# A decoder block's first MLP projection with stacked operands, its opening in smaller steps, and one merge step placed two background steps later

## The chip, the cores and the metric

The kernel runs on one core of a Trainium2 chip. The metric is the device time of one execution in microseconds (us), the median of several runs. TensorE appears in the profile as PE (matmuls) and PEld (loads of the stationary operand), VectorE as DVE, ScalarE as ACT, GpSimd as POOL; SP issues most transfers.

## The reference

One layer of a hybrid decoder trunk on 256 tokens of width 2048, with a memory of 256 tokens, all in float32:

```
proj = rmsnorm(x) @ w_in            # q,k,v,gates of three branches, 3 x 2048 merge gates
oa, ob = gated_deltanet(...), hgrn2(...)
oc = memory_attention(cq, rmsnorm(mem), w_kv)
merged = ga*(oa @ w_br_a) + gb*(ob @ w_br_b) + gc*(oc @ w_br_c)
x = x + rmsnorm(merged @ w_out)
h2 = rmsnorm(x)
m = square(relu(h2 @ w_mlp_in)) @ w_mlp_out     # 2048 -> 8192 -> 2048
x = x + rmsnorm(m)
```

## The kernel before

**Precision by splitting.** Every float32 operand of a large product is split into a rounded part and a remainder (hi and lo, both float32r), and a product is the sum of three matmuls: hi·hi, hi·lo and lo·hi. Weights arrive by `load_w` (L137): one DMA of two k-tiles by 512 columns (512 KB) on SP's queue, a cast on ACT to `wh` (L144), and a subtraction on DVE to `wl` (L146). The pools `w`, `wh` and `wl` have four buffers each, so a load, a cast or a subtraction waits for the one four groups earlier to be done with.

**Units.** `unit` (L154) computes 512 output columns for all 256 tokens. It goes over the k-tiles in groups of two. In kind "x" the activations are stationary and the weights move: per k-tile and block of 128 tokens three matmuls that each move 512 columns (L180, L181, L182). In kind "w" the weights are stationary and the activations move: per k-tile and block of 128 output columns three matmuls that each move 256 tokens (L187, L188, L189), so the output comes transposed, as the next product needs it. An x unit over 16 k-tiles has 96 matmuls, a w unit 192. Both accumulate in one PSUM tile of two banks from a pool of two (`pmm`), or, with `split`, in two tiles of one bank each from the pool `pbp` of four banks that the transposes also use.

**Order of the work.** The program is written as units in sequence, with generators (`bg`) as background work: after each group `tick` runs as many background steps as a rate says, one step lasting to the next `yield`. Within that, a scheduler sets the order of each engine's instructions; PE, ACT and DVE each work through theirs in order.

**The opening** (L223 to L409): four units compute the memory's values (two x units) and keys (two w units). During the first of them `load_mem` (L241) brings `mem` in four chunks of 512 columns and `transpose_chunk` (L208) transposes each into `memh` and `meml` (L216, L200, L201). Then `gen_start` (L316) forms the norm of `mem`, loads `x` in four chunks and some small parameters, forms the sum of squares of `x` (L311), scales `x` by its norm (L373) and transposes it (L216) into `hh` and `hl`; `gen_masks` (L260) builds masks. All later projections need `hh` and `hl`.

**Merge.** In `branch` (L780), when a merged chunk `mg` is complete (L792), `gen_merge` (L767) transposes it (L774) in two background steps. The product with `w_out` needs all four chunks.

**MLP.** `mlp_in` (L1002) makes 1024 hidden columns in two units, `mlp_out` (L1047) multiplies them back in four x units over 8 k-tiles and adds into `yacc`. This is done eight times, `mlp_in(e)` ahead of `mlp_out(e-1)`. Of the 16 units of `mlp_in` the first is an x unit, the other 15 are w units: L187 to L189 with the operands `h2h` and `h2l`. Each ends with relu on ACT (L1008), a squaring on DVE (L1010), a cast on ACT (L205) and a subtraction on DVE (L206).

Of the kernel before, what the change touches and what calls it, by code (L numbers as in the profile page):

```python
# [41 lines left out]
def tile_trunk(ctx: ExitStack, tc, a):  # L42
# [4 lines left out]
    wp = ctx.enter_context(tc.tile_pool(name="wp", bufs=4))  # L47
    hp = ctx.enter_context(tc.tile_pool(name="hp", bufs=8))
    gp = ctx.enter_context(tc.tile_pool(name="gp", bufs=25))
# [9 lines left out]
    def nm(s):  # L59
        cnt[0] += 1  # L60
        return f"{s}_{cnt[0]}"
# [3 lines left out]

    def h4(name):
        return hp.tile([P, 4, S], F32R, tag="h", name=nm(name))

# [12 lines left out]

    warm = const("warm", [P, 16])
    V.memset(warm, 0.0)
    A.copy(warm, warm)
    ident = const("ident", [P, P])
# [24 lines left out]

    load_gcol(["g_mem"], 0, nc.sync.dma_start)

# [41 lines left out]
    def unit(kind, act, nk, src, c0, r0=0, pre=None, order=None, split=False, post=None):  # L154
# [52 lines left out]

    def transpose_chunk(src, tiles, c, col0):  # L208

        hi, lo = tiles  # L210
        for half in range(2):
            pt = bank("tr")
            for q in range(2):
                for t in range(NT):
                    kk = half * 2 + q
                    T.transpose(pt[:, q * S + t * P:q * S + (t + 1) * P],  # L216
                                src[:, t, kk * P:(kk + 1) * P], ident)
# [23 lines left out]
    def load_mem(k0):  # L241
        if k0 % 4:
            return
        c = k0 // 4
        t = g4("mem", (P, NT, 512))
        nc.sync.dma_start(t, mem_r[:, :, c * 512:(c + 1) * 512])
        hi, lo = g4("memh", (P, 4, S), F32R), g4("meml", (P, 4, S), F32R)
        transpose_chunk(t, (hi, lo), c, 0)
        mem_s.append(t)
        memT.append((hi, lo))  # L250

# [53 lines left out]

    def sumsq(chunks, name):
        st = small(name, 8)
        for c, t in enumerate(chunks):
            for k in range(NT):
                j = g4("junk")  # L310
                A.activation(j[:, 0:512], t[:, k, :], AF.Square, accum_out=st[:, k * 4 + c:k * 4 + c + 1])  # L311
        ss = small(name + "s", NT)
        V.tensor_reduce(out=ss, in_=st.rearrange("p (k c) -> p k c", k=NT), axis=AX.X, op=ALU.add)
        return ss

    def gen_start():  # L316
        ss = sumsq(mem_s, "ssm")
        yield
        r = rstd_of(ss, NT, D)
        V.tensor_copy(rsm, r)  # L320
# [7 lines left out]
        xs = []  # L328
        for c in range(4):
            t = g4("x", (P, NT, 512))  # L330
            nc.sync.dma_start(t, x_r[:, :, c * 512:(c + 1) * 512])
            xs.append(t)
        yield
        load_gcol(["g_pre_mix", "g_pre_mlp"], 16, adma)
        crow = const("crow", [96, P])
# [3 lines left out]
        V.tensor_copy(ccol, pc[:, 0:96])  # L339
        yield  # L340
        lrow = const("lrow", [8, P])
        adma(lrow, a["lb_raw"][0].rearrange("(c p) -> c p", p=P))
        pl = bank("pl")
        T.transpose(pl[:, 0:8], lrow, ident[0:8, 0:8])
# [18 lines left out]
        adma(alog, a["a_log"][0:1, :].to_broadcast([P, 8]))  # L363
        adma(dtb, a["dt_bias"][0:1, :].to_broadcast([P, 8]))
        A.activation(alog, alog, AF.Exp)
        yield
        ssx = sumsq(xs, "ssx")
        yield
        rx = rstd_of(ssx, NT, D)
        for c in range(4):  # L370
            hT[c] = (h4("hh"), h4("hl"))
            for t in range(NT):
                V.tensor_scalar(out=xs[c][:, t, :], in0=xs[c][:, t, :], scalar1=rx[:, t:t + 1],  # L373
                                scalar2=None, op0=ALU.mult)
            transpose_chunk(xs[c], hT[c], c, 16)
            yield

    ccol = const("ccol", [P, 96])
# [8 lines left out]
    for u in range(2):  # L387
        ps = unit("x", act_of(memT), KT, w_kv, 1024 + 512 * u, pre=load_mem if u == 0 else None)
        if u == 0:
            bg.append(gen_start())  # L390
            bg.append(gen_masks())
# [374 lines left out]

    def gen_merge(j):  # L767
        hi, lo = g4("mgh", (P, 4, S), F32R), g4("mgl", (P, 4, S), F32R)
        for hh in range(2):
# [166 lines left out]
    last = [(g, None) for g in range(4)] + [(g, t) for t in range(NT) for g in range(4, 8)]  # L936
    h2T = []

# [23 lines left out]
    for c in range(4):  # L962
        y = g4("y1", (P, NT, 512))
        ys.append(y)
        if c < 3:
            ps = unit("x", mact, KT, a["w_out"][0], 512 * c)
            for t in range(NT):
                mix_evac(y, c, t, ps[:, t * 512:(t + 1) * 512])
        else:
            h2T.extend((h4("h2h"), h4("h2l")) for _ in range(4))  # L970
# [31 lines left out]
    def mlp_in(e):  # L1002
        mt = []
        for u in range(2):
            kind = "x" if e == 0 and u == 0 else "w"
            ps = unit(kind, h2act, KT, a["w_mlp_in"][0], e * 1024 + u * 512, order=first if kind == "x" else None)
            r = g4("relu")
            A.activation(r, ps, AF.Relu)  # L1008
            hi, lo = g4("mh", (P, 4, S), F32R), g4("ml", (P, 4, S), F32R)
            V.scalar_tensor_tensor(out=r, in0=ps, scalar=0.0, in1=r, op0=ALU.max, op1=ALU.mult)  # L1010
            if kind == "x":
                for hh in range(2):
# [34 lines left out]
    def mlp_out(e, mt):  # L1047
        for c in range(4):
            args = ("x", act_of(mt), 8, a["w_mlp_out"][0], c * 512, e * 8)
            if e == NE - 1 and c == 3:  # L1050
# [5 lines left out]
                continue  # L1056
            ps = unit(*args)
            if e == 0:
                yacc[c] = g4("yacc", (P, NT, 512))
                A.copy(yacc[c], ps.rearrange("p (t n) -> p t n", t=NT))  # L1060
            elif e < NE - 1:
                V.tensor_tensor(out=yacc[c], in0=ps.rearrange("p (t n) -> p t n", t=NT), in1=yacc[c], op=ALU.add)
            else:
                for t in range(NT):
                    mlp_evac(c, t, ps[:, t * 512:(t + 1) * 512])

# [22 lines left out]
```

## Time and profile before

| what | value |
|---|---|
| runs | 1867.44, 1868.84, 1868.90 us; median 1868.84 |
| the profiled execution | 1866.51 us; span 1864.8 us from first to last instruction |
| mean granted TensorE clock | 0.996 of full |
| PE busy | 1831.4 us (98%), 11174 matmuls |
| PEld busy | 1641.5 us (88%) |
| DVE busy | 1088.3 us (58%) |
| ACT busy | 895.2 us (48%) |
| POOL busy | 45.5 us (2%) |
| moved by DMA | 333.63 MB, mean 179 GB/s |

The times in the rows of a profile are from the start of the span. Matmuls overlap, so the duration of one (0.28 us, say) is longer than the distance to the next; what a matmul costs in a stream is read from the distance of two starts. The page's line PEclk gives the clock that TensorE was granted, in tenths of full speed.

### The profile page before, as it was taken

The page shows a single profiled execution, that of the slowest core. Times are in us where ns is not written, and L with a number is a line of the kernel's source. Part 1 is how long each engine was busy: PE and PEld are TensorE (multiplying, and loading weights), DVE is VectorE, ACT ScalarE, POOL GpSimd, SP SyncE. Part 2 cuts the span into 40 slices and gives each one's busy share as a digit, 9 for nine tenths or more (in the row PEclk, how much of TensorE's full clock was granted, in tenths as well). Part 3 has the DMA queues.
Part 4 walks back from the last instruction along what each step waited for, and adds up shares of the span by engine and source line. Part 5 has one row for each costly group of instructions (what it writes and reads, how often), then busy time and mean ns, then how long its engine had stood idle before and what let it go on. Part 6 is the DMA issues. An engine that isn't in the chain of part 4 may idle for free.

```text
span 1864.8 us, 27445 instructions
## 1 busy us (share of the span) xinstructions
PE 1831.4 (98%) x11174; PEld 1641.5 (88%) x11174; DVE 1088.3 (58%) x1328; ACT 895.2 (48%) x1079; POOL 45.5 (2%) x70
## 2 busy tenths in 40 slices
PE   7899999999999999999999999999999999999997
PEld 6799999988899898888888787989898989898986
DVE  4655577764863685875455557554555554545556
ACT  5544555444545565654444445544444444444433
POOL 1100000200110000000000000000000000000000
PEclk9899999999999999999999999999999999999999
DMA  6566656664584555555665765656566655666653
GB/s 206 183 192 172 169 148 171 181 183 124 169 210 132 157 169 148 161 155 179 187 196 183 247 193 178 184 186 189 191 187 190 189 189 184 192 183 193 185 194 127
DMA packets 174383, 333.63 MB, mean 179 GB/s; under 512 B 13080, under 2 KB 13744, under 8 KB 174000
## 3 DMA queue, kind: packets, MB, share of 16 engines
q1 hardware_dynamic: 168736, 325.11, 57.7%
q10 hardware_dynamic: 4496, 4.54, 0.8%
q0 software_dynamic: 1024, 2.23, 0.6%
q8 instruction: 87, 1.43, 0.3%
q14 instruction: 40, 0.33, 0.1%
HBM read 329.60 MB, written 2.23 MB: 178 GB/s over the span
## 4 chain that ended last, share of the span: by engine, by line
PE 58%; issue 39%; DVE 2%; DMA 0%; ACT 0%; POOL 0%; SPq 0%; DVEq 0%; POOLq 0%; ACTq 0%
PE mm L180 12%; PE mm L182 12%; PE mm L181 12%; PE mm L187 6%; PE mm L189 6%; PE mm L188 5%; PE pa L865 1%; PE pw L696 1%; PE pzt L701 1%; DMA mem<-in_mem 0%; DVE wl L146 0%; PE tr L216 0%; DVE x L1044 0%; PE ab L483 0%; PE mgT L774 0%
## 5 line engine op out<-in xcount | busy, mean ns | idle before, releaser
L146 DVE TENSOR_TENSOR wl<-w,wh 128x1024 fp32r<-128x1024 f32 x608 | 741.5, 1223 | 620.7 <-ACT wh L144 619.8
L144 ACT CAST wh<-w 128x1024 fp32r<-128x1024 f32 x608 | 636.9, 1050 | 838.7 <-PE mm L182 447.6
L187 PE MATMUL mm<-h2h,wh 128*128 128x256 f32 x960 | 271.7, 283 | 0.0
L188 PE MATMUL mm<-h2l,wh 128*128 128x256 f32 x960 | 271.7, 283 | 0.0
L189 PE MATMUL mm<-h2h,wl 128*128 128x256 f32 x960 | 271.7, 283 | 0.0
L180 PE MATMUL mm<-wh,hh 128*128 128x512 f32 x576 | 228.5, 397 | 0.0
L182 PE MATMUL mm<-wh,hl 128*128 128x512 f32 x576 | 224.9, 390 | 0.0
L181 PE MATMUL mm<-wl,hh 128*128 128x512 f32 x576 | 224.5, 390 | 0.0
L187 PE MATMUL mm<-hh,wh 128*128 128x256 f32 x768 | 218.8, 285 | 0.0
L189 PE MATMUL mm<-hh,wl 128*128 128x256 f32 x768 | 217.4, 283 | 0.1
L188 PE MATMUL mm<-hl,wh 128*128 128x256 f32 x768 | 217.3, 283 | 0.0
L180 PE MATMUL mm<-wh,mh 128*128 128x512 f32 x512 | 199.3, 389 | 0.0
L181 PE MATMUL mm<-wl,mh 128*128 128x512 f32 x512 | 199.3, 389 | 0.0
L182 PE MATMUL mm<-wh,ml 128*128 128x512 f32 x512 | 199.2, 389 | 0.0
L188 PEld LDWEIGHTS mm<-h2l,wh 128*128 128x128 f32 x960 | 184.3, 192 | 0.3
L187 PEld LDWEIGHTS mm<-h2h,wh 128*128 128x128 f32 x960 | 184.3, 192 | 0.3
L189 PEld LDWEIGHTS mm<-h2h,wl 128*128 128x128 f32 x960 | 184.3, 192 | 0.0
L187 PEld LDWEIGHTS mm<-hh,wh 128*128 128x128 f32 x768 | 147.3, 192 | 0.2
L188 PEld LDWEIGHTS mm<-hl,wh 128*128 128x128 f32 x768 | 147.3, 192 | 0.2
L189 PEld LDWEIGHTS mm<-hh,wl 128*128 128x128 f32 x768 | 147.2, 192 | 0.3 <-DVE wl L146 0.3
L182 PEld LDWEIGHTS mm<-wh,hl 128*128 128x128 f32 x576 | 108.1, 188 | 23.1
L181 PEld LDWEIGHTS mm<-wl,hh 128*128 128x128 f32 x576 | 108.4, 188 | 20.9
(360 smaller groups left out, 2359.6 us busy)
## 6 DMA issues: line engine op xcount, KB each, us to landing
w<-in_w_in SPq DMA_DIRECT2D x240, 512.0 KB, 3.7
w<-in_w_mlp_in SPq DMA_DIRECT2D x128, 512.0 KB, 3.7
w<-in_w_mlp_out SPq DMA_DIRECT2D x128, 512.0 KB, 3.6
w<-in_w_kv_mem SPq DMA_DIRECT2D x32, 512.0 KB, 5.6
w<-in_w_out SPq DMA_DIRECT2D x32, 512.0 KB, 3.7
w<-in_w_br_c SPq DMA_DIRECT2D x16, 512.0 KB, 4.4
w<-in_w_br_a SPq DMA_DIRECT2D x16, 512.0 KB, 3.7
w<-in_w_br_b SPq DMA_DIRECT2D x16, 512.0 KB, 3.6
```

Of the source, the lines that this page charges most:

```text
L144: i_hi = A.copy(wh[:, 0:n, 0:width], w[:, 0:n, 0:width])
L146: i_lo = V.tensor_tensor(out=wl[:, 0:n, 0:width], in0=w[:, 0:n, 0:width], in1=wh.bitcast(F32)[:, 0:n, 0:width], op=ALU.subtract)
L180: T.matmul(o, st, wh[:, j, :], start=kt == 0, stop=False)
L181: T.matmul(o, st, wl[:, j, :], start=False, stop=False)
L182: T.matmul(o, sl, wh[:, j, :], start=False, stop=kt == nk - 1)
L187: T.matmul(o, sh, ah, start=kt == 0 and c % 2 == 0, stop=False)
L188: T.matmul(o, sh, al, start=False, stop=False)
L189: T.matmul(o, sl, ah, start=False, stop=kt == nk - 1 and c % 2 == 1)
L696: T.matmul(pw[:, b * 64:(b + 1) * 64], U[:, b, :], half_view(X, s, False)[:, b], start=True, stop=True)
L701: T.matmul(pzt[:, b * 64:(b + 1) * 64], W[:, b, :], half_view(XT, s, True)[:, b], start=True, stop=True)
L865: T.matmul(pa[:, b * 64:(b + 1) * 64], kp[:, h, t * P:(t + 1) * P], qp[:, b * 64:(b + 1) * 64], start=True, stop=True)
```

## The change

Three things change. **First**, the 15 w units of `mlp_in` become `unit_stacked`. The hi and lo parts of an activation chunk now lie in one tile (`h8`, shape 128 x 2 x 4 x 256; half as many buffers of twice the size), so that one matmul with `wh` stationary moves both, 512 columns, into a whole bank: hi·hi in its first half, hi·lo in its second. A second matmul with `wl` moves the 256 columns of the hi part into the first half. The four blocks of output columns take a bank each, alternately the four of `pbp` and the two double ones of `pmm`. The two halves are added at the end by ACT and DVE, in place of relu on ACT. The first two of the four units of each `mlp_out` now take their banks from `pbp`, and their results are evacuated by blocks of 128 tokens.

```
+    def unit_stacked(pairs, nk, src, c0, ps):
+        for g in range(nk // KG):
+            k0 = g * KG
+            wh, wl = load_w(src, k0, KG, c0)
+            for j in range(KG):
+                kt = k0 + j
+                both = pairs[kt // 4][:, :, kt % 4, :]
+                for c in range(4):
+                    T.matmul(ps[c], wh[:, j, c * P:(c + 1) * P], both, start=kt == 0, stop=False)
+                    T.matmul(ps[c][:, 0:S], wl[:, j, c * P:(c + 1) * P], both[:, 0, :], start=False, stop=kt == nk - 1)
+            tick()
...
-                split_psum(r.rearrange("p (c s) -> p c s", c=4), hi, lo)
+                if u == 0:
+                    ps = [bank("mm") for _ in range(4)]
+                else:
+                    ps = []
+                    for _ in range(2):
+                        both = pmm.tile([P, 1024], F32, tag="mm", name=nm("mm"))
+                        ps.extend((both[:, 0:512], both[:, 512:1024]))
+                unit_stacked(h2B, KT, a["w_mlp_in"][0], c0, ps)
+                r4 = r.rearrange("p (c s) -> p c s", c=4)
+                for c in range(4):
+                    A.copy(r4[:, c, :], ps[c][:, S:2 * S])
+                    V.tensor_tensor(out=r4[:, c, :], in0=ps[c][:, 0:S], in1=r4[:, c, :], op=ALU.add)
+                V.scalar_tensor_tensor(out=r, in0=r, scalar=0.0, in1=r, op0=ALU.max, op1=ALU.mult)
+                split_psum(r4, hi, lo)
...
-            ps = unit(*args)
+            ps = unit(*args, split=c < 2)
```

**Second**, the opening. The first chunk of `mem` comes in two halves by two DMAs, and every chunk is transposed in two calls, one per half. The load of `g_mem` goes from SP's queue to ACT's, ahead of ACT's table load. The sums of squares of `x` are formed chunk by chunk in steps of their own, the chunks of `x` are loaded one per step, the mask steps alternate with them, and each chunk is scaled one step ahead of its transposes.

```
-        ssx = sumsq(xs, "ssx")
-        yield
-        rx = rstd_of(ssx, NT, D)
+        load_x()
+        sumsq_chunk(xs[0], st, 0)
+        yield
...
+        next(masks)
+        yield
...
+        sumsq_chunk(xs[3], st, 3)
+        yield
+        next(masks)
+        yield
+        rx = rstd_of(sumsq_of(st, "ssx"), NT, D)
...
+        scale(0)
+        yield
         for c in range(4):
-            hT[c] = (h4("hh"), h4("hl"))
+            if c < 3:
+                scale(c + 1)
+            hc = h8("hh")
+            hT[c] = (hc[:, 0], hc[:, 1])
             transpose_chunk(xs[c], hT[c], c, 16)
             yield
+        yield from masks
```

ACT, second chunk of `mem` (tile `mem_185` before, `mem_186` now; `tr` are its transposes in PSUM, `memh` the hi part). Before:

```order
8 L144 CAST wh_169<-w_167 128x1024
9 L144 CAST wh_209<-w_207 128x1024
10 L200 ACTIVATE memh_187<-tr_189,gcol 128x256
11 L144 CAST wh_227<-w_225 128x1024
12 L200 ACTIVATE memh_187<-tr_189,gcol 128x256
13 L144 CAST wh_267<-w_265 128x1024
14 L200 ACTIVATE memh_187<-tr_198,gcol 128x256 x2
```

The same place of ACT's program now:

```order
9 L145 CAST wh_170<-w_168 128x1024
10 L145 CAST wh_201<-w_199 128x1024
11 L145 CAST wh_228<-w_226 128x1024
12 L145 CAST wh_259<-w_257 128x1024
13 L145 CAST wh_286<-w_284 128x1024
14 L215 ACTIVATE memh_187<-tr_190,gcol 128x256
15 L215 ACTIVATE memh_187<-tr_217,gcol 128x256
```

The four activations that make `memh` of the second chunk stood among the casts, and now stand behind the casts of the fifth and sixth weight group. On PE, seven of the chunk's eight transposes stood ahead of the first chunk's matmuls, and two do now.

PE, the transposes of `x` (L216, chunks `x_416` and `x_418`), inside the second values unit (`mm_397`, last two weight groups). Before:

```order
193 L180 MATMUL mm_397<-wh_599,memh_303 128x512
194 L216 MATMUL tr_579<-ident,x_416 128x128
195 L216 MATMUL tr_588<-ident,x_416 128x128
196 L181 MATMUL mm_397<-wl_601,memh_303 128x512
197 L216 MATMUL tr_579<-ident,x_416 128x128 x3
198 L216 MATMUL tr_588<-ident,x_416 128x128 x3
199 L182 MATMUL mm_397<-wh_599,meml_304 128x512
200 L216 MATMUL tr_619<-ident,x_418 128x128 x4
201 L216 MATMUL tr_628<-ident,x_418 128x128 x4
202 L180 MATMUL mm_397<-wh_639,memh_303 128x512
```

PE now, the first chunk of `x` (`x_417`), inside the first keys unit (`mm_617`, last two weight groups):

```order
350 L189 MATMUL mm_617<-meml_246,wh_798 128x256
351 L190 MATMUL mm_617<-memh_245,wl_800 128x256
352 L231 MATMUL tr_829<-ident,x_417 128x128 x4
353 L231 MATMUL tr_838<-ident,x_417 128x128 x4
354 L188 MATMUL mm_617<-memh_303,wh_849 128x256
355 L189 MATMUL mm_617<-meml_304,wh_849 128x256
```

The transposes of `x` have moved out of the second values unit into the two keys units, eight at a time with 24 matmuls of a weight group between two batches.

**Third**, the generator for the last merged chunk begins with two empty steps.

```
     def gen_merge(j):
+        if j == 3:
+            yield
+            yield
```

PE, the end of the last branch unit (`mm_9332`, later `mm_9329`) and the start of the first `w_out` unit (`mm_9421`, later `mm_9418`). Before:

```order
5521 L182 MATMUL mm_9332<-wh_9389,ol_8196 128x512
5522 L180 MATMUL mm_9421<-wh_9424,mgh_8712 128x512
5523 L774 MATMUL mgT_9460<-ident,mg_5375 128x128 x4
5524 L774 MATMUL mgT_9485<-ident,mg_5375 128x128 x4
5525 L181 MATMUL mm_9421<-wl_9426,mgh_8712 128x512
```

The same place now:

```order
5489 L183 MATMUL mm_9329<-wh_9386,ol_8193 128x512
5490 L181 MATMUL mm_9418<-wh_9421,mgh_8709 128x512
5491 L825 MATMUL mgT_9493<-ident,mg_5372 128x128 x4
5492 L825 MATMUL mgT_9518<-ident,mg_5372 128x128 x4
5493 L182 MATMUL mm_9418<-wl_9423,mgh_8709 128x512
```

On PE nothing has moved here: the eight transposes still stand behind the first matmul of the `w_out` unit. On ACT the two casts that follow them stand behind one weight cast more, and on DVE the first of the two subtractions does.

More of the change, by code (lines that the diff above doesn't have):

```diff
@@ L64, in g4, with h8 @@
         return gp.tile(list(shape), dt, tag="g", name=nm(name))
-    def h4(name):
-        return hp.tile([P, 4, S], F32R, tag="h", name=nm(name))
+    def h8(name):
+        return hp.tile([P, 2, 4, S], F32R, tag="h", name=nm(name))
     def small(name, n=16):
@@ L109, in load_gcol @@
         V.tensor_copy(gcol[:, c0:c0 + n], pg[:, 0:n])
-    load_gcol(["g_mem"], 0, nc.sync.dma_start)
+    load_gcol(["g_mem"], 0, adma)
+    warm = const("warm", [P, 16])
+    V.memset(warm, 0.0)
+    A.copy(warm, warm)
     bg = []
@@ L206, in split_psum, with transpose_chunk @@
         V.tensor_tensor(out=lo, in0=ps, in1=hi.bitcast(F32), op=ALU.subtract)
-    def transpose_chunk(src, tiles, c, col0):
+    def transpose_chunk(src, tiles, c, col0, halves=(0, 1)):
         hi, lo = tiles
-        for half in range(2):
+        for half in halves:
             pt = bank("tr")
@@ L241, in load_mem @@
     def load_mem(k0):
[L242 to L250, printed above, removed]
+        c, half = k0 // 4, k0 % 4 // 2
+        if half == 0:
+            mem_s.append(g4("mem", (P, NT, 512)))
+            memT.append((g4("memh", (P, 4, S), F32R), g4("meml", (P, 4, S), F32R)))
+        t = mem_s[c]
+        cols = [slice(half * 256, half * 256 + 256)] if c == 0 else [slice(0, 512)] * (1 - half)
+        for sl in cols:
+            nc.sync.dma_start(t[:, :, sl], mem_r[:, :, c * 512 + sl.start:c * 512 + sl.stop])
+        transpose_chunk(t, memT[c], c, 0, (half,))
     mgt, mlt, caus = const("mgt", [P, P]), const("mlt", [P, P]), const("caus", [P, P])
@@ L304, in tile_trunk, with sumsq_chunk, sumsq_of @@
     hT = [None] * 4
[L306 to L311, printed above, removed]
+    def sumsq_chunk(t, st, c):
+        for k in range(NT):
+            j = g4("junk")
+            A.activation(j[:, 0:512], t[:, k, :], AF.Square, accum_out=st[:, k * 4 + c:k * 4 + c + 1])
+    def sumsq_of(st, name):
         ss = small(name + "s", NT)
@@ L316, in gen_start @@
     def gen_start():
-        ss = sumsq(mem_s, "ssm")
+        st = small("ssm", 8)
+        for c, t in enumerate(mem_s):
+            sumsq_chunk(t, st, c)
         yield
-        r = rstd_of(ss, NT, D)
+        r = rstd_of(sumsq_of(st, "ssm"), NT, D)
         V.tensor_copy(rsm, r)
@@ L328, in gen_start, with load_x @@
         xs = []
-        for c in range(4):
+        def load_x():
+            c = len(xs)
             t = g4("x", (P, NT, 512))
@@ L364, in gen_start, with scale @@
         adma(dtb, a["dt_bias"][0:1, :].to_broadcast([P, 8]))
+        yield
+        st = small("ssx", 8)
+        load_x()
+        sumsq_chunk(xs[0], st, 0)
+        yield
         A.activation(alog, alog, AF.Exp)
+        next(masks)
         yield
-        ssx = sumsq(xs, "ssx")
+        load_x()
+        sumsq_chunk(xs[1], st, 1)
         yield
-        rx = rstd_of(ssx, NT, D)
-        for c in range(4):
-            hT[c] = (h4("hh"), h4("hl"))
+        next(masks)
+        yield
+        sumsq_chunk(xs[2], st, 2)
+        yield
+        next(masks)
+        yield
+        sumsq_chunk(xs[3], st, 3)
+        yield
+        next(masks)
+        yield
+        rx = rstd_of(sumsq_of(st, "ssx"), NT, D)
+        def scale(c):
             for t in range(NT):
@@ L969, in tile_trunk @@
         else:
-            h2T.extend((h4("h2h"), h4("h2l")) for _ in range(4))
+            h2B.extend(h8("h2h") for _ in range(4))
+            h2T.extend((b[:, 0], b[:, 1]) for b in h2B)
             ps = unit("x", mact, KT, a["w_out"][0], 512 * c, order=last, split=True,
@@ L1004, in mlp_in @@
         for u in range(2):
-            kind = "x" if e == 0 and u == 0 else "w"
-            ps = unit(kind, h2act, KT, a["w_mlp_in"][0], e * 1024 + u * 512, order=first if kind == "x" else None)
+            c0 = e * 1024 + u * 512
+            hi, lo = g4("mh", (P, 4, S), F32R), g4("ml", (P, 4, S), F32R)
             r = g4("relu")
[L1008 to L1011, printed above, removed]
+            if e == 0 and u == 0:
+                ps = unit("x", h2act, KT, a["w_mlp_in"][0], c0, order=first)
+                A.activation(r, ps, AF.Relu)
+                V.scalar_tensor_tensor(out=r, in0=ps, scalar=0.0, in1=r, op0=ALU.max, op1=ALU.mult)
                 for hh in range(2):
```

31 lines of the change are left out of this document (18 added, 13 removed).

## The prediction

> **What bounds the kernel now.** I read the page first: busy times and the chain that ended last.
>
> ```profile
> span 1864.8 us, 27445 instructions
> PE 1831.4 (98%) x11174; PEld 1641.5 (88%) x11174; DVE 1088.3 (58%) x1328; ACT 895.2 (48%) x1079; POOL 45.5 (2%) x70
> PE 58%; issue 39%; DVE 2%; DMA 0%; ACT 0%; POOL 0%; SPq 0%; DVEq 0%; POOLq 0%; ACTq 0%
> ```
>
> PE is busy for 98% of the span, and the chain is PE and its issue for 97%. So two things count: what PE's stream costs, and where PE stands still. Next, the stream in the timeline of PE: first and last start of a run of 54 narrow matmuls (256 columns, 18 triples of an MLP w unit), then of 93 wide ones (512 columns, 31 triples of an x unit).
>
> ```profile
> 1214.64 0.28 PE L187 MATMUL mm<-h2h,wh 128*128 128x256 f32 x1
> ...
> 1221.12 0.28 PE L187 MATMUL mm<-h2h,wh 128*128 128x256 f32 x1
> ```
>
> ```profile
> 1499.97 0.39 PE L180 MATMUL mm<-wh,mh 128*128 128x512 f32 x1
> ...
> 1521.05 0.39 PE L180 MATMUL mm<-wh,mh 128*128 128x512 f32 x1
> ```
>
> Narrow: 6.48 us / 54 = 0.1200 us from start to start. Wide: 21.08 / 93 = 0.2267. Two narrow ones cost 0.2400 for the same 512 columns, so a straight line through both prices has 0.0133 us per instruction that no column pays for.
>
> Then, where PE stands still: its waits, the windows around them, and PE's timeline on both sides of the longest.
>
> ```profile
> PE tr L216 <- DMA mem<-in_mem: 5.0, 2, 2.8
> PE tr L216 <- issue: 4.9, 2, 3.9
> ...
> PE mgT L774 <- DVE mg L792: 2.4, 1, 2.4
> ...
> PE mT L1017 <- DVE relu L1010: 0.7, 1, 0.7
> ```
>
> ```profile
> 60.90:84.13 23.23, 16.98 (x92) 15.17 (x92) 17.18 (x38) 15.72 (x32) 0.71 (x1) 0.78 0.25 89
> 84.13:124.80 40.67, 40.67 (x341) 40.67 (x341) 25.07 (x33) 15.73 (x15) 4.33 (x6) 1.00 0.68 208
> ```
>
> ```profile
> 60.70 0.39 PE L180 MATMUL mm<-wh,memh 128*128 128x512 f32 x1
> 64.98 0.66 PE L216 MATMUL tr<-ident,x 128*128 128x128 f32 x2 [3.89 <-issue]
> ...
> 80.93 0.41 PE L189 MATMUL mm<-memh,wl 128*128 128x256 f32 x1
> 81.14 0.41 PE L187 MATMUL mm<-memh,wh 128*128 128x256 f32 x1
> ```
>
> All waits of note lie in the opening, but for one of 2.4 us at the last merged chunk. The stretch from 60.90 to 84.13 is the bad one: the mean granted clock is 0.78 there, and behind each standstill matmuls start at 0.21 instead of 0.12. From 84.13 on PE is full.
>
> **The stacked projection.** A w unit has 16 x 4 = 64 triples. Each becomes one wide and one narrow matmul: 0.2267 + 0.1200 = 0.3467 us for 0.3600. 15 units x 64 x 0.0133 = **12.8 us less**, all on the path, since PE is the bound here. The trace has no alternation of wide and narrow, so I bound it. Nothing gained if the wide one, whose moving operand is now two pieces 4 KB apart, is priced as two narrow ones (0.3600). At the other end the narrow one costs half a wide one (0.1133): 960 x 0.0200 = 19.2 us. I take the straight line, since an operand in two pieces already runs at its price, the Gram matmuls with a moving operand of 2 x 128 columns:
>
> ```profile
> 328.47 0.28 PE L417 MATMUL kk<-kqh 128*128 128x256 f32 x1
> 328.59 0.28 PE L418 MATMUL kk<-kql,kqh 128*128 128x256 f32 x1
> ```
>
> 0.12 us, as in one piece. [...]
>
> The end of a unit gets heavier. What it costs now, the nearest rows for 256 columns out of PSUM, and how full ACT and DVE are in such a unit (third and fourth busy time behind the length):
>
> ```profile
> L1010 DVE SCALAR_TENSOR_TENSOR relu<-mm,relu 128x1024 f32<-128x1024 f32 x16 | 19.5, 1217 | 0.0
> L206 DVE TENSOR_TENSOR ml<-relu,mh 128x1024 fp32r<-128x1024 f32 x15 | 18.3, 1218 | 0.0
> L1008 ACT ACTIVATE relu<-mm 128x1024 f32<-128x1024 f32 x16 | 16.4, 1022 | 0.0
> L205 ACT CAST mh<-relu 128x1024 fp32r<-128x1024 f32 x15 | 15.7, 1046 | 0.0
> ...
> L522 DVE SCALAR_TENSOR_TENSOR cv<-mm,ccol,cv 128x255 f32<-128x255 f32 x24 | 11.5, 478 | 3.3 <-ACT cv L519 3.2
> ...
> L519 ACT ACTIVATE cv<-mm,ccol 128x256 f32<-128x256 f32 x24 | 11.3, 472 | 5.4 <-DVE cv L522 5.4
> ```
>
> ```profile
> 1206.00:1229.00 23.00, 23.00 (x194) 23.00 (x193) 12.07 (x10) 10.26 (x10) 0.00 (x0) 1.00 0.58 186
> ```
>
> ACT goes from 1.02 + 1.05 to 4 x 0.47 + 1.05 = 2.93 us (+0.9), DVE from 2.44 to 4 x 0.48 + 2.44 = 4.35 (+1.9). Of 23 us, 13 and 11 are idle, so I cost it at nothing. Queued behind these instructions are the casts and subtractions for the next groups, but three groups (3 x 8 x 0.3467 = 8.3 us of PE) lie ready in the four buffers, and the added chain is some 5.4 us (1.88 + 1.22 + 1.05 + 1.22). The banks change hands as well: a stacked unit takes all four of `pbp` or both tiles of `pmm`, and the unit after it takes the other pool, so each has a whole unit to be emptied. One exception is the first stacked unit, which needs the tile that the x unit ahead of it just filled; there PE's order has seven pairs (2.4 us) and the transposes of `relu` first, and the wait of before (0.7 us, on `mT`) stays what it was. The evacuation of `mlp_out` in halves is the same work in more instructions under the same cover. In the stretch between `w_out` and the MLP a few rows of ACT and DVE change places; its waits were small, and I put ±1 us on it.
>
> **The opening, transposes of `x`.** At full rate the stretch from 60.90 to 84.13 holds 32 transposes, 14 wide and 46 narrow matmuls (92 in all). A batch of eight transposes takes 0.87 us:
>
> ```profile
> 406.32 0.87 PE XT L689 x8
> ```
>
> 32 x 0.109 + 14 x 0.2267 + 46 x 0.12 = 12.2 us; 11.1 of the 23.2 are lost. The cause is on ACT and DVE (timelines): ACT waits for a parameter's DMA, then forms all eight squares ahead of the next casts, and DVE can scale `x` only behind them.
>
> ```profile
> 55.45 0.21 ACT L365 ACTIVATE alog<-alog 128x8 f32<-128x8 f32 x1 [4.36 <-DMA alog<-in_a_log]
> ...
> 58.08 0.62 ACT L311 ACTIVATE junk<-x 128x512 f32<-128x512 f32 x1
> ...
> 63.08 2.92 ACT L144 CAST wh<-w 128x1024 fp32r<-128x1024 f32 x3
> ```
>
> ```profile
> 64.40 1.68 DVE L373 TENSOR_SCALAR x<-x,r 128x512 f32<-128x512 f32 x4 [0.82 <-POOL r L228]
> ```
>
> PE stood in its order before a transpose of `x` from 61 to 64.98. Now the transposes come one to two units later, when `x` has long been scaled, so that wait and those behind it go. What is late next: the ACT wait for `alog` stays, and four squares instead of eight stand ahead of the cast for the last group of the second values unit. The eight took 63.08 - 58.08 = 5.0 us, so that cast begins at about 58.08 + 2.5 = 60.6, and with 1.05 for itself and 1.23 for its subtraction all is ready at 62.9. PE wants it at 60.70 + 3 x 0.2267 = 61.4 and can do one matmul without the subtraction: 1.3 us lost. Four switches to transposes and back cost 0.1 each. Gain 11.1 - 1.3 - 0.4 = **9.4 us** (5 if the heavy DVE stretch of the keys units, with all `hl`, holds up each batch by 1 us; 11 if nothing is late).
>
> **The opening, chunks of `mem`.** PE's timeline at the second chunk:
>
> ```profile
> 13.06 1.75 PE L216 MATMUL tr<-ident,mem 128*128 128x128 f32 x7 [2.19 <-DMA mem<-in_mem]
> ...
> 20.42 0.27 PE L216 MATMUL tr<-ident,mem 128*128 128x128 f32 x1
> 20.45 0.48 PE L180 MATMUL mm<-wh,memh 128*128 128x512 f32 x1
> ```
>
> It will still land at about 13 us: the same bytes stand ahead of it on SP's queue, and the `g_mem` row that left the queue is small. At 20.4 PE lost nearly nothing, since seven transposes were done. Now six of the eight come there, and the activations behind two casts that wait for PE, as those of the third chunk did before:
>
> ```profile
> 26.00 1.04 PE L216 MATMUL tr<-ident,mem 128*128 128x128 f32 x8
> 26.25 1.05 ACT L144 CAST wh<-w 128x1024 fp32r<-128x1024 f32 x1 [1.68 <-PE mm L182]
> ...
> 29.00 0.51 PE L182 MATMUL mm<-wh,meml 128*128 128x512 f32 x1 [0.55 <-DVE meml L201]
> ```
>
> From 26.00 to 29.00 PE did eight transposes and two matmuls, 0.87 + 0.45 = 1.3 us of work: 1.7 lost. So **1.7 us more** (0 to 3). The third chunk's DMA moves on SP behind four more weight loads, the last of which waits for a buffer:
>
> ```profile
> 20.28 0.37 SPq L139 DMA_DIRECT2D w<-in_w_kv_mem  x1
> ```
>
> ```profile
> 3.83 9.18 DMA mem<-in_mem
> ```
>
> The first row is the ninth weight load; the chunk goes out right behind it, at some 20.8, and is wanted at 26.00 + 1.7 = 27.7, so 6.9 us cover it. The second row, from the chain, is the transfer of the second chunk: 9.2 us in the crowd of the start. At 20 us less is under way, so I count nothing, and put up to 2 us into the range.
>
> **The merged chunk.** The 2.4 us wait stays: on PE its transposes stand where they stood, behind the first matmul of `w_out`. 0 us; 2.4 less only if the order were another.
>
> **Sum.** -12.8 - 9.4 + 1.7 = -20.5 us. The profiled execution took 1866.51 us (span 1864.8), 2.3 below the median of the runs, 1868.84; from that median the forecast is **1848.3 us**.
>
> **Rivals.** (1) *The projection gains nothing*: the two-piece operand makes a wide matmul two narrow ones, or the fixed part is not per instruction. Against it is the Gram row; for it, no alternating stream in the trace. Then only the opening counts: 1868.8 - 7.7 = 1861.1. Chance 0.07. [...] (2) *The opening gives back what it saves*: PE still stands before a transpose of `x`, or the late third chunk takes a new wait at 26 to 30 us and the clock falls as at 61. For it: DVE is the fullest engine there. 1868.8 - 12.8 = 1856. Chance 0.12. (3) *Slower*: PE waits at the start of each of the 15 stacked units or of the unit behind for the banks, which now take eight instructions (4 copies at 0.47 and the last addition, 2.4 us) to empty. 15 x 2.4 = 36 us, 1884; it decides from 20.5 / 15 = 1.4 us per unit. Against it: the pools alternate. Chance 0.03.
>
> **How the numbers follow.** The forecast and its near variants have 0.78. Low end: projection 16 and opening 10.5, 1842; high end: opening at its small end and rival (2), and a little over, 1858; beyond lie rivals (1) and (3) and part of the unknown price. About 0.2% (3.7 us) is what a measurement of this kernel can tell from no change, so "same" is 1865.1 to 1872.6: only (1) and (2) together get there, 0.03 out of their chances. Slower is rival (3), 0.03; faster 0.94.
>
> **What would show it.** In the projection: starts of wide matmuls 0.347 apart from pair to pair, 22.2 us per unit, PE without a gap at unit ends. In the opening: no wait of 3.9 us on a transpose, clock 1.00 between 20 and 115 us, a stall of some 1.7 us at 20 us and one near 62, and the first use of `hh` at about 117 instead of 124.9:
>
> ```profile
> 124.91 0.28 PE L187 MATMUL mm<-hh,wh 128*128 128x256 f32 x1
> ```
>
> A wait of 2.4 us on `mgT` remains. Wrong would be pairs at 0.36, a clock under 1.0 between 60 and 115 us, or waits for PSUM at unit ends.

## The result, and the profile after

| | runs (us) | median | against before |
|---|---|---|---|
| before | 1867.44, 1868.39, 1868.84, 1868.90 | 1868.62 | |
| after | 1851.34, 1852.16, 1855.03, 1856.05 | 1853.6 | 0.9921 [0.9904, 0.9938] |

The change makes the kernel 15.0 us faster where 20.5 were forecast. The profiled execution of after took 1855.03 us, span 1853.3, which is 11.5 less than the span of before; it is one of the two longer runs of after, for which the record has a mean granted clock of 0.997 and 0.996, against 0.998 in the two shorter ones. First the sums: busy times of the page, then the waits of PE.

```profile
PE 1822.6 (98%) x10214; PEld 1588.2 (86%) x10214; DVE 1111.0 (60%) x1412; ACT 901.6 (49%) x1128; POOL 44.2 (2%) x70
```

```profile
PE tr L231 <- DMA mem<-in_mem: 4.3, 3, 2.3
PE gcol L106 <- DMA grow<-in_g_mem: 4.0, 1, 4.0
PE mgT L825 <- DVE mg L843: 2.4, 1, 2.4
PE mT L1069 <- DVE relu L1063: 2.1, 1, 2.1
PE mm L181 <- ACT wh L145: 1.9, 1, 1.9
PE mm L182 <- DVE wl L147: 1.8, 2, 1.6
```

PE has 960 matmuls fewer and is as full as before. The wait of 3.9 us on a transpose of `x` is gone, the 2.4 us on `mgT` are there as before, and the wait on `mT` has grown from 0.7 to 2.1 us. Of the 1.8 us on `wl`, 1.6 are one wait in the first unit of the MLP, at 1129.67 us, where before had 0.65. No wait stands at the ends of the stacked units: from 1160 us on PE never stands still for more than 0.06 us.

Next, the opening: a window of PE from 60 us to the first use of `hh` (busy times, then granted clock, DMA share and GB/s), and that first use, 124.91 in before.

```profile
60.00:117.40 57.40, 57.40 (x452) 56.02 (x451) 40.91 (x67) 33.60 (x56) 3.76 (x7) 1.00 0.65 210
```

```profile
117.47 0.28 PE L188 MATMUL mm<-hh,wh 128*128 128x256 f32 x1
```

PE is busy in all of it at full clock: 7.4 us won, 7.7 forecast.

Last, the stacked stream. PE's timeline at two places, the first and last wide matmul of 31 in the first stretch of pairs and of 30 in the second:

```profile
1189.57 0.40 PE L206 MATMUL mm<-h2h,wh 128*128 128x512 f32 x1
...
1199.97 0.40 PE L206 MATMUL mm<-h2h,wh 128*128 128x512 f32 x1
...
1299.25 0.40 PE L206 MATMUL mm<-h2h,wh 128*128 128x512 f32 x1
...
1309.50 0.40 PE L206 MATMUL mm<-h2h,wh 128*128 128x512 f32 x1
```

The same two instructions have two paces. In the first stretch a pair takes 10.40 / 30 = 0.3467 us, which is the forecast to the last digit; in the second 10.25 / 29 = 0.3534. The first stretch (three units in a row, up to 1222 us) keeps the one pace throughout, each of the six later ones (two units each) the other, on their mean 0.3537.

By places in the traces the 11.5 us of the two profiled executions fall like this:

| stretch | before ends at | after ends at | difference in it |
|---|---|---|---|
| start to first use of `hh` | 124.91 | 117.47 | -7.4 |
| to first use of `h2h` (end of the mix) | 1130.59 | 1122.98 | -0.2 |
| to first use of `mh` (first units of the MLP) | 1229.04 | 1222.50 | +1.1 |
| to the last matmul | 1853.60 | 1842.10 | -5.0 |

In this pair of executions the opening came as forecast; the MLP did not.

### The profile page after: what moved, and what is told of

It is laid out like the page before. It is cut to its first block, busy times and chain, and to the rows that moved or that the text cites. A ratio compares the mean times of both kernels' runs of the same rounds, so it can differ in the third digit from the quotient of the medians.

```text
span 1853.3 us, 25652 instructions
## 1 busy us (share of the span) xinstructions
PE 1822.6 (98%) x10214; PEld 1588.2 (86%) x10214; DVE 1111.0 (60%) x1412; ACT 901.6 (49%) x1128; POOL 44.2 (2%) x70
## 3 DMA queue, kind: packets, MB, share of 16 engines
q0 software_dynamic: 1024, 2.23, 0.7%
## 4 chain that ended last, share of the span: by engine, by line
PE 59%; issue 38%; DVE 1%; DMA 0%; ACT 0%; POOL 0%; SPq 0%; DVEq 0%; POOLq 0%; ACTq 0%
PE mm L181 12%; PE mm L183 12%; PE mm L182 12%; PE mm L188 6%; PE mm L190 6%; PE mm L189 6%; PE pa L916 1%; PE pw L744 1%; PE pzt L749 1%; DMA mem<-in_mem 0%; DVE wl L147 0%; DVE x L1109 0%; PE tr L231 0%; PE ab L531 0%; PE mgT L825 0%
## 5 line engine op out<-in xcount | busy, mean ns | idle before, releaser
L147 DVE TENSOR_TENSOR wl<-w,wh 128x1024 fp32r<-128x1024 f32 x608 | 741.1, 1222 | 598.6 <-ACT wh L145 595.3
L206 PE MATMUL mm<-h2h,wh 128*128 128x512 f32 x960 | 339.1, 399 | 0.0
L181 PE MATMUL mm<-wh,hh 128*128 128x512 f32 x576 | 228.5, 397 | 0.0
L183 PE MATMUL mm<-wh,hh 128*128 128x512 f32 x576 | 225.0, 391 | 0.0
L188 PE MATMUL mm<-hh,wh 128*128 128x256 f32 x768 | 218.9, 285 | 0.0
L189 PE MATMUL mm<-hh,wh 128*128 128x256 f32 x768 | 217.4, 283 | 0.0
L188 PEld LDWEIGHTS mm<-hh,wh 128*128 128x128 f32 x768 | 147.4, 192 | 0.2
L189 PEld LDWEIGHTS mm<-hh,wh 128*128 128x128 f32 x768 | 147.4, 192 | 0.2
L183 PEld LDWEIGHTS mm<-wh,hh 128*128 128x128 f32 x576 | 108.1, 188 | 23.1
L181 PEld LDWEIGHTS mm<-wh,hh 128*128 128x128 f32 x576 | 108.3, 188 | 20.6
L183 PEld LDWEIGHTS mm<-wh,ml 128*128 128x128 f32 x512 | 96.1, 188 | 20.2
```

Of the source, the lines that this page charges most:

```text
L147: i_lo = V.tensor_tensor(out=wl[:, 0:n, 0:width], in0=w[:, 0:n, 0:width], in1=wh.bitcast(F32)[:, 0:n, 0:width], op=ALU.subtract)
L181: T.matmul(o, st, wh[:, j, :], start=kt == 0, stop=False)
L183: T.matmul(o, sl, wh[:, j, :], start=False, stop=kt == nk - 1)
L188: T.matmul(o, sh, ah, start=kt == 0 and c % 2 == 0, stop=False)
L189: T.matmul(o, sh, al, start=False, stop=False)
L206: T.matmul(ps[c], wh[:, j, c * P:(c + 1) * P], both, start=kt == 0, stop=False)
```

## The experiments

Every ratio is to runs of before on the same chip, with its 95% interval. Durations are PE's, from start to start, unless another engine is named.

**1. One piece instead of two.** Is the wide matmul dear because its moving operand lies in two pieces?

```
-        return hp.tile([P, 2, 4, S], F32R, tag="h", name=nm(name))
+        return hp.tile([P, 4, 2, S], F32R, tag="h", name=nm(name))
...
-                both = pairs[kt // 4][:, :, kt % 4, :]
+                both = pairs[kt // 4][:, kt % 4, :, :]
```

> Kernel after, but the high and low parts of one group of 128 rows of the activations lie side by side, so that the wide matmul of a pair (512 columns) reads one contiguous piece instead of two pieces of 256 columns 4 KB apart. The changed kernel's pair takes 0.3536 us (28 pairs in 9.90 us), not the 0.3467 forecast: 0.236 for the wide one, 0.118 for the narrow one. Theory A, the wide matmul is streamed as two pieces of 256 columns, each with a price of its own: now 0.2267 + 0.118 = 0.345 us per pair, 960 x 0.009 = 8 us less than after, about 1846. Rival B, the narrow and wide matmuls hinder each other in alternation (the weight load behind a narrow one), or the change of PSUM bank costs: 0.3536 stays, no change, about 1854.

1853.0 us, 0.9920 [0.9907, 0.9934]: no change. PE's timeline of this kernel, 31 wide matmuls of the first stretch:

```profile
1189.49 0.40 PE L206 MATMUL mm<-h2h,wh 128*128 128x512 f32 x1
...
1200.09 0.40 PE L206 MATMUL mm<-h2h,wh 128*128 128x512 f32 x1
```

10.60 / 30 = 0.3533 with a contiguous operand: theory A falls. And here the first stretch too has the slower pace.

**2. Two pieces close together.** As 1, with the tile `[P, 4, 2, S + 8]` and the last eight columns of each piece unused.

> As the contiguous kernel, but with 8 unused columns behind each piece, so the wide matmul's operand is again two pieces, 1056 bytes apart instead of 4 KB. Theory A, two pieces cost two prices: pair 0.3536 us as in after, about 1854. Theory A2, it is the distance of 4 KB and not the number of pieces: pair 0.345, about 1846. Rival B (alternation or banks): 0.3536, about 1854, and then the contiguous kernel does not gain either.

1856.66 us, 0.9940 [0.9927, 0.9952], about 3 us slower than after. Two rows of the second stretch, 35 wide matmuls:

```profile
1298.93 0.39 PE L206 MATMUL mm<-h2h,wh 128*128 128x512 f32 x1
...
1310.86 0.39 PE L206 MATMUL mm<-h2h,wh 128*128 128x512 f32 x1
```

11.93 / 34 = 0.3509, a little better than either, so the layout takes some 0.002 us off a pair. What it loses lies elsewhere: the x units that take `hh` as stationary operand became slower, the same line in after and here (duration minimum, median, maximum in ns):

```profile
L182 PE MATMUL mm<-wl,hh x576: 387/389/398, 248.3 to 1019.5; 128*128 128x512 f32 x192
```

```profile
L182 PE MATMUL mm<-wl,hh x576: 389/396/400, 245.2 to 1022.7; 128*128 128x512 f32 x192
```

The median is 7 ns longer, and from the first use of `hh` to that of `h2h` this kernel takes 1011.7 us where kernel 1 takes 1007.1 (mean granted clock of the whole executions 0.997 and 0.998). So where an operand lies does matter, but not in the way that theory A has it. Why, no run here says.

**3. Four wide, then four narrow.**

```
                 for c in range(4):
                     T.matmul(ps[c], wh[:, j, c * P:(c + 1) * P], both, start=kt == 0, stop=False)
+                for c in range(4):
                     T.matmul(ps[c][:, 0:S], wl[:, j, c * P:(c + 1) * P], both[:, 0, :], start=False, stop=kt == nk - 1)
```

> Kernel after, but in each group of 128 rows the four wide matmuls of the stacked projection come first and the four narrow ones behind them, so that wide and narrow alternate four times less often. The operand stays in two pieces 4 KB apart. Theory A (two pieces): 4 x 0.236 + 4 x 0.118 = 1.414 us per four pairs as before, no change, about 1854. Rival B1 (alternation): 4 x 0.2267 + 4 x 0.12 with one change of width, 1.387 us, 240 x 0.027 = 6.6 us less, about 1847. Rival B2 (a change of bank costs): now all eight matmuls change bank instead of four, so slower by a few us if anything.

1851.46 us, 0.9912 [0.9899, 0.9926]. Groups of four wide ones, six groups apart (the end of the view cuts one matmul off the last):

```profile
1299.92 1.09 PE L206 MATMUL mm<-h2h,wh 128*128 128x512 f32 x4
...
1308.34 0.86 PE L206 MATMUL mm<-h2h,wh 128*128 128x512 f32 x3
```

8.42 / 6 = 1.403 us per four pairs instead of 4 x 0.3534 = 1.414. Fewer changes of width cost less, as B1 says, but not the 1.387 that it forecast. B2 (a change of bank) falls: every matmul changes bank now.

**4. Grouped and contiguous**, 1 and 3 together.

> The grouped kernel (four wide matmuls, then four narrow ones) with the wide operand in one contiguous piece. In the grouped kernel four pairs took 1.403 us, wide to wide 0.2334, where a wide matmul of an x unit takes 0.2267. Theory C, a wide operand in two pieces does cost 0.007 us when no narrow one stands between, so contiguous wide ones run at 0.2267: four pairs 1.383, 240 x 0.02 = 4.8 us less than the grouped kernel, about 1846.5. Rival D, the pieces cost nothing and the wide matmuls of this projection are dear for their roles (weights stationary, activations moving) or their change of bank: 0.2334 and 1.403 us stay, about 1851.

1850.92 us, 0.9911 [0.9897, 0.9924]: as 3, also pair by pair (wide to wide 0.2334 in both). Theory C falls, and with it the last form of "the two pieces cost something".

**5. Only wide ones.** The narrow matmul becomes a wide one, so that the product of both low parts is computed as well.

```
-                    T.matmul(ps[c][:, 0:S], wl[:, j, c * P:(c + 1) * P], both[:, 0, :], start=False, stop=kt == nk - 1)
+                    T.matmul(ps[c], wl[:, j, c * P:(c + 1) * P], both, start=False, stop=kt == nk - 1)
```

> Kernel after, but the narrow matmul of each pair is a wide one too (the low part of the weights times high and low part, which adds the product of the two low parts; nothing is left out). 960 matmuls grow from 256 to 512 columns, so it is slower by design; wanted is the pitch of wide matmuls of this kind with no narrow one among them. Rival B1, mixing of widths costs: 0.2267 us from start to start, 0.4533 per pair, 960 x 0.1 = 96 us over after, about 1950. Rival D, roles or operands of this projection cost: 0.233 to 0.236 us, 0.466 to 0.472 per pair, 108 to 114 us over after, about 1965.

1948.7 us in one run, as B1 has it. 23 wide matmuls of line 206, with 22 of line 207 between them:

```profile
1304.92 0.39 PE L206 MATMUL mm<-h2h,wh 128*128 128x512 f32 x1
...
1314.89 0.39 PE L206 MATMUL mm<-h2h,wh 128*128 128x512 f32 x1
```

9.97 / 44 = 0.2266 us, with the operand in two pieces 4 KB apart, the weights stationary, and in all stretches of the MLP. So neither the pieces nor the roles cost anything; the price appears only where wide and narrow stand in one stream. Theory D falls. Nor is it that every matmul loads new weights, since the pure streams do that too (PEld has as many instructions as PE, 11174 of each in before). Whether it is the change of width itself that costs, or a load that runs behind a matmul of the other width, no run separates.

**6. Eight wide, then eight narrow.** The wide matmuls of both k-tiles of a weight group, then the narrow ones.

> Kernel after, but in each group of weights all eight wide matmuls (two groups of 128 rows, four banks) come first and the eight narrow ones behind them. Eight pairs took 8 x 0.3536 = 2.829 us in after and 2 x 1.403 = 2.806 grouped by four; at the prices in pure runs (0.2267 and 0.1200) they would take 2.774. Theory B1a, each change between the widths costs: the surplus of the groups of four, 0.016 per four pairs, is now paid once per eight: 2.790 us, 120 x 0.039 = 4.7 us less than after. Rival B1b, every matmul of a mixed unit pays: 2.806, as in groups of four, 2.8 us less than after. Either way about 1849 to 1851.

1849.28 us, 0.9897 [0.9882, 0.9911].

```profile
1299.84 2.00 PE L206 MATMUL mm<-h2h,wh 128*128 128x512 f32 x8
1301.68 1.12 PE L211 MATMUL mm<-h2h,wl 128*128 128x256 f32 x8
1302.63 2.00 PE L206 MATMUL mm<-h2h,wh 128*128 128x512 f32 x8
```

2.79 us per eight pairs, some 0.018 over the pure prices (2.774), where four pairs had 0.016: this fits B1a, where the surplus is paid about once per change of width, and not B1b, which has 2.806. In these groups the first five wide matmuls take 0.228 to 0.235 and the last three 0.2267, averaged over the later stretches.

**7. The opening alone.** Opening and merge of after, `mlp_in` and `mlp_out` of before.

> Opening and merge of after, MLP of before (three narrow matmuls, no stacked projection). Theory: the opening is worth 7.4 us (first use of hh at 117.5 instead of 124.9) and nothing of it is given back: 7.4 us under before, about 1860.5, and the stacked projection is worth the rest, some 6 to 7 us. Rival: the lead of the opening is given back at a later wait, so this kernel is within 2 us of before (1866 to 1868) and the projection is worth nearly the whole 15 us.

1859.18 us, 0.9955 [0.9942, 0.9969], 8.1 us under before. The opening keeps its gain to the end, and some 7 of the 15 us are left for the rest.

**8. Whole chunks of mem.** `load_mem` as in before, the rest as in after.

> Kernel after, but the chunks of mem are loaded and transposed whole, as in before (both halves of a chunk ahead of its first matmul), with the transposes of x where after has them. Theory: the halves cost 3.75 us in after (third chunk's transposes at 29.75 instead of 26.00 us), so 2 to 4 us less than after, about 1850, and first use of hh at 113.7 to 115.5. Rival: the stall belongs to the landing of the chunks and comes back in another place: no change, first use of hh at 117.5, about 1853.6.

1852.57 us, 0.9919 [0.9906, 0.9933]: by the times no difference to after. The traces say more. First use of `hh` here, and in kernel 4, which has the opening of after unchanged:

```profile
113.69 0.28 PE L188 MATMUL mm<-hh,wh 128*128 128x256 f32 x1
```

```profile
115.64 0.28 PE L188 MATMUL mm<-hh,wh 128*128 128x256 f32 x1
```

The same opening that came to 117.47 in the profile of after came to 115.64 here. The reason is the pace of PE at its start (PE's timeline; after, then kernel 4):

```profile
16.06 0.63 PE L181 MATMUL mm<-wh,memh 128*128 128x512 f32 x1
...
18.62 0.63 PE L181 MATMUL mm<-wh,memh 128*128 128x512 f32 x1
```

```profile
16.44 0.39 PE L181 MATMUL mm<-wh,memh 128*128 128x512 f32 x1
...
18.48 0.39 PE L181 MATMUL mm<-wh,memh 128*128 128x512 f32 x1
```

Six matmuls in 2.56 us (0.427 each) against nine in 2.04 (0.227): in that execution of after PE came to full pace at 19.2 us, in kernel 4 at 16.1, in before at 15.8. In the 14 profiles of this study the point lies anywhere between 15.6 and 19.2. Eleven of them have the opening of after: in the six that reach full pace by 16.6 the first use of `hh` is at 115.4 to 116.0, in the five that do so from 18.3 on at 116.7 to 117.5. Against an execution that starts alike, the halves of the chunks cost 115.6 - 113.7 = 1.9 us (forecast 1.7), and the whole opening of after wins 124.9 - 115.6 = 9.3.

**9. The first stacked unit** in the banks of the other pool, and the transposes of the first `relu` behind it.

> Kernel after, but the first stacked unit takes its banks from the other pool than the unit ahead of it, and the transposes of the first relu go behind it on TensorE, so TensorE runs on into that unit instead of waiting 2.10 us for relu (DVE) before its transposes; the pools of all later units change places with it. Theory: in after this wait and the lower clock behind it (granted mean 0.66 from 1155 to 1160 us) cost 2 to 3.5 us, where before waited 0.7; expect 2 to 3.5 us less than after, about 1850.5, no wait on mT, clock 1.00 there. Rival: the wait is made up elsewhere, or the transposes take a new wait behind the second unit: no change, about 1854.

1851.89 us, 0.9915 [0.9902, 0.9929]; against after that is inside the spread. The place itself did what was expected; the same window of after and of this kernel:

```profile
1150.00:1176.00 26.00, 23.90 (x130) 20.73 (x129) 13.45 (x12) 11.30 (x13) 0.00 (x0) 0.93 0.65 195
```

```profile
1150.00:1176.00 26.00, 26.00 (x150) 22.49 (x149) 15.15 (x15) 12.46 (x15) 0.00 (x0) 1.00 0.74 230
```

150 matmuls instead of 130, no idle time, full clock. But the profile of this kernel has lower clock at another place, behind the wait on `mgT`:

```profile
1032.80:1036.20 3.40, 3.36 (x12) 2.50 (x11) 3.40 (x4) 1.04 (x2) 0.00 (x0) 0.63 0.54 150
```

**10. Without the two empty steps.**

> Kernel after without the two empty background steps ahead of the last merged chunk. TensorE's order is row by row the same. Theory: no change, about 1853, and the wait of 2.4 us on mgT stays. Rival: the two steps move the casts or subtractions of that chunk on ACT and DVE and are worth up to the 2.4 us: 1855.5.

1853.48 us, 0.9919 [0.9904, 0.9934], wait on `mgT` 2.4: no change, as forecast for that part. Its first stacked stretch ran at 0.3533 us per pair and that of after at 0.3467, with the same order on PE. Its trace shows best what lower clock is: the window behind that wait, here and in after (third value from the end: granted clock).

```profile
1032.80:1036.20 3.40, 3.08 (x12) 2.79 (x13) 3.40 (x5) 1.66 (x3) 0.00 (x0) 0.50 0.23 44
```

```profile
1029.40:1032.80 3.40, 1.80 (x8) 1.14 (x7) 1.76 (x2) 0.61 (x1) 0.00 (x0) 1.00 1.02 377
1032.80:1036.20 3.40, 2.61 (x15) 2.11 (x16) 3.40 (x4) 1.51 (x3) 0.00 (x0) 1.00 0.17 44
1155.87:1159.28 3.41, 3.41 (x14) 3.12 (x15) 2.40 (x3) 1.17 (x2) 0.00 (x0) 0.50 0.78 219
```

The same wait of 2.4 us is followed by half clock in one kernel and not in the other; after pays instead behind the wait on `mT`.

**11. A standstill ahead of later stretches.** One small DVE instruction ahead of each of four stretches of the stacked stream, for which PE must wait at three of them. Here stretches are numbered by the block of 1024 hidden columns: the first stretch from above is the second half of block 1 and block 2, the second is stretch 3, the last is 8.

```
+    def hold(e):
+        gate = yacc[2 if e == 3 else 3][:, 1, 0:1]
...
+        one = h2B[0][:, 0, 0, 0:1]
+        V.scalar_tensor_tensor(out=one, in0=gate, scalar=0.0, in1=one.bitcast(F32), op0=ALU.mult, op1=ALU.add)
```

> In after the first 180 pairs behind the wait of 2.10 us ran at the forecast 0.3467 us (16 instructions in 2.773 us from 1162 to 1218 us), and all later stacked stretches, which start behind wide matmuls without a wait, at 0.3536. In the kernel with whole chunks of mem (wait 1.5 us) the first stretch also ran at 0.3467, in the contiguous one (wait 0.63) at 0.3536. This is kernel after with one small VectorE instruction ahead of four of the later stretches (it adds zero times another value to one column of the activations and changes nothing), which TensorE must wait for: at stretch 4 it hangs on a value that is long there (no wait), at stretch 5 on the evacuation of the last unit (a wait of some 1.5 us), at 6 and 7 on that and one more VectorE instruction of 512 and 1024 columns (some 2.2 and 2.8 us); stretches 3 and 8 are as in after. Theory S, a standstill of over 1 us right ahead of it sets the faster pace: 0.3467 per pair in stretches 5, 6 and 7 and 0.3536 in 3, 4 and 8. Rival R, the pace belongs to the stretch (its place in the program) and not to the wait: 0.3536 in all but the first. In all some 6 us of waits are added and up to 2.7 us of pace won, about 1857.

1866.0 us in one run; the waits came to 2.67, 3.19 and 3.46 us, each with half clock behind it, and so dearer than expected. The paces, first and last wide matmul of some 10 us in stretches 5 (29 of them), 6 (29) and 7 (30):

```profile
1459.87 0.40 PE L206 MATMUL mm<-h2h,wh 128*128 128x512 f32 x1
...
1469.75 0.40 PE L206 MATMUL mm<-h2h,wh 128*128 128x512 f32 x1
...
1549.92 0.40 PE L206 MATMUL mm<-h2h,wh 128*128 128x512 f32 x1
...
1559.81 0.40 PE L206 MATMUL mm<-h2h,wh 128*128 128x512 f32 x1
...
1639.63 0.39 PE L206 MATMUL mm<-h2h,wh 128*128 128x512 f32 x1
...
1649.68 0.39 PE L206 MATMUL mm<-h2h,wh 128*128 128x512 f32 x1
```

0.3529, 0.3532 and 0.3466. Rival R falls, since stretch 7 changed its pace and is at the same place of the program as in after. Theory S falls as it was put: two of three long waits left the slower pace. The undisturbed stretches 3, 4 and 8 ran at 0.353 as expected.

**12. Together:** whole chunks of `mem` (8), the first unit's banks (9) and groups of eight (6).

> Kernel after with three edits together: chunks of mem whole (lead of some 1.8 us at the first use of hh), the first stacked unit in the other pool's banks with the transposes of relu behind it (2.1 us of waiting and a possible period at half clock less), and eight wide matmuls before eight narrow ones (2.8 to 4.7 us). If they add up: 6.5 to 8.5 us less than after, 1845 to 1847; if leads are given back at the 2.4 us wait on mgT or in lower clock behind it, about 1849.

1846.8 us, 0.9885 [0.9868, 0.9901], 20.6 us less than the 1867.38 of before on that chip: the fastest of the study, at the slow end of what was expected. Behind `mgT` its profile has the wait of 2.4 us and half clock from 1030.78 to 1034.20, so a part of the lead may be given back there.

## Why the prediction was right and where it was not

**The bound and the direction** held: PE is the bound in both kernels, and instructions taken from its stream came off the time.

**The projection, -12.8, is the step that failed:** "I take the straight line, since an operand in two pieces already runs at its price". The half about the pieces was right (runs 1, 4 and 5). The straight line was read from two pure streams, and a stream that mixes both widths has a price of its own: 0.3467 us per pair in three stretches (the first of after and of run 8, one of run 11), 0.353 in all others that alternate (0.351 in the layout of run 2). In the profile of after the six later stretches, 768 pairs, won 5.0 us, 0.0065 each instead of 0.0133; the first, 192 pairs, had the forecast pace. Together that is 5.0 + 2.5 = 7.5 us, and some 6.2 in an execution where the first stretch is slow as well, as in run 1. The prediction had said that no alternating stream was in the trace and had bounded the term by 0 and 19.2. Shown is that the surplus isn't the pieces, the roles of the operands or the change of bank, and that fewer changes of width make it smaller than in the slow pace (runs 3 and 6). The distance of the pieces and the row length, changed together in run 2, account for some 0.002 of it. What stays open is what chooses between the paces. It isn't the place in the program (runs 10 and 11). All three fast stretches stand behind a wait of 1.5 us or more, but two others behind waits of 2.67 and 3.19 us were slow, so a wait does not settle it.

**The transposes of x, -9.4,** came out larger, some 11.2: the opening won 9.3 in executions that start alike, with 1.9 lost at the second and third chunk of `mem`. The wait of 1.3 us that the prediction put near 62 us did not come (PE has no gap over 0.1 us between 33 and 1031 us), and with it goes most of the difference. This is the upper end that it gave, "11 if nothing is late". A switch to transposes and back cost about the 0.1 us put for it: in after the first matmul behind eight of them starts at 86.01 and the next at 86.21, 0.20 us for 0.12. That the profiled pair shows 7.4, so near to the 7.7 forecast for the whole opening, is luck: the late start of that execution took the surplus away again.

**The chunks of mem, +1.7,** measured 1.9 by run 8. The profile of after shows 3.75 at the third chunk's transposes (29.75 for 26.00); kernel 4, with the same opening and an early start, has them at 27.93. So 1.9 are the halves, and the other 1.8 come with the late start, which no edit set.

**The first stacked unit** was to keep its wait of 0.7 us. It was 2.1 in the profile of after and 0.3 to 1.7 in the other kernels that have it there. ACT's timeline, before and then after:

```profile
1158.03 1.05 ACT L144 CAST wh<-w 128x1024 fp32r<-128x1024 f32 x1 [1.74 <-DMA w<-in_w_mlp_in]
1158.98 1.02 ACT L1008 ACTIVATE relu<-mm 128x1024 f32<-128x1024 f32 x1
```

```profile
1152.32 1.05 ACT L145 CAST wh<-w 128x1024 fp32r<-128x1024 f32 x1 [1.97 <-DMA w<-in_w_mlp_in]
1153.27 1.01 ACT L1062 ACTIVATE relu<-mm 128x1024 f32<-128x1024 f32 x1
```

In both kernels the relu stands behind a cast that waits for its weights; that order is not new. What differs is when the weights land, seen from PE. In before the cast began 0.09 us ahead of the first matmul of the unit behind (1158.12), in after 1.22 us later than it (1151.10). In all twelve profiles that have this wait, PE waits 0.8 to 0.9 us longer than the cast is late, and the lateness runs from -0.53 to 1.22 us. So a transfer sets this wait. The prediction spoke of the order on PE and not of what stands ahead of the relu on ACT. Why the weights land later in some executions, no run shows. In the table this wait, the one of 1.6 us on `wl` and the half clock make the stretch 1.1 us longer than in before, although its pairs ran at the forecast pace outside the half clock.

**The merge, 0,** was right (run 10). **Rival (3)**, waits for banks at unit ends, is excluded: no such wait in any trace. **Rival (2)**, the opening gives its gain back, is excluded by run 7. **Rival (1)**, nothing gained from the projection, is false as well, but lies as near to the truth as the forecast: about half of the term came.

In all: 6.2 to 7.5 us come from the projection where 12.8 were forecast, 9.3 from the opening where 7.7 were, and 1 to 2 are lost again in half clock and waits at the merge and the first stacked unit. That is 13.5 to 15.8, and 15.0 was measured. The terms come from several executions, whose starts alone differ by up to 2 us, so this is an account and no proof. That the time lies inside the range is in part luck: the opening made up 1.6 us of what the projection fell short of, and the upper end, 1858, had been put together from an opening that fails and not from a dearer stream.

## What to carry to other kernels

Two instruction widths that are each measured in a pure stream do not give the price of a stream that mixes them; group equal ones (eight and eight won some 4 us here against the slower pace) or measure the mixed stream itself. A gain of a few microseconds on TensorE can be given back behind a wait (half clock for 3.41 us in after), so compare places in the trace between executions that started alike, and not two spans. Of an instruction that PE waits for, look also at what stands ahead of it on its own engine.

## What the runs showed of the hardware

While PE has work, the lower clock comes in pieces of 3.41 us at 0.50: in the profile of after one, from 1155.87 to 1159.28; in before one from 80.69 to 84.11 and, twice as long, one from 63.63 to 70.45. The piece behind `mgT` in kernel 12, from 1030.78 to 1034.20, is as long. In the profiles of before and after the changes of the clock lie whole multiples of 3.413 us apart: in before, from the start of full pace at 15.84 on, 47.79, 6.83, 10.24 and 3.41 us (14, 2, 3 and 1 times it), in after, from 19.23 on, 1136.64 and 3.41 us (333 and 1 times). The start of full pace differs in kernels that begin nearly alike: 15.7 us in kernel 5, 16.1 in kernel 4, 18.4 in kernel 6, 19.2 in after. The wait of 2.4 us on `mgT` was followed by lower clock in kernels 4, 8, 9, 10 and 12 (0.50 to 0.70 in the 3.4 us where most of it lies), and not in before, after and kernels 6 and 7 (1.00).

If these multiples are taken as a grid through the whole of a trace, which is an assumption where no change of clock shows it, the waits on `mgT` and `mT` can be sorted by how much of them falls into one piece of 3.413 us. Half clock followed where this was 2.0 us or more (2.0 in kernel 10, 2.10 on `mT` in after, 2.3 in kernels 8 and 12), and did not where it was 1.5 or less (1.5 in kernel 6, 1.32 in before). Between the two it does not decide: 1.90 us was followed by half clock in kernel 4, but 1.79 and 1.90 were not in after and kernel 7. In kernel 4 the eight transposes behind the wait lie in the same piece, in the other two they don't. This is read from the traces and was not tried by moving the wait.

Full-rate matmuls of 512 and 256 columns took 0.2267 and 0.1200 us in the pure streams of the MLP, the wide ones with the moving operand in one piece or in two. The straight line through both leaves 13.3 ns per instruction. It is no rule for every stream: the wide matmuls of run 2 with `hh` stationary ran slower (median duration 396 ns for 389).
